# First block's gated layers: the high part of w against both parts of x in one product of 512 columns

## The chip, the cores and the metric

The kernel runs on one NeuronCore of a Trainium2 chip. The metric is device time in microseconds (us) of one execution; lower is better. Three executions of the kernel before gave 2074.72, 2075.59 and 2077.48 us; the median, 2075.59, is the time that the change is measured against.

In this document PE is the matrix engine (TensorE) and PEld its loading of weights, DVE is VectorE, ACT is ScalarE, POOL is GpSimd, SP is SyncE (it issues most DMAs). PSUM is the memory that PE writes to, in 8 banks of 512 float32 columns for each partition.

## The reference, cut to what matters

Two transformer blocks of two layers each run one after the other over x, 256 tokens of width 1024, in float32. The change touches only the gated layers of the first block: two in each of its two layers, four in all.

```python
D_MODEL, SEQ, D_FF, DEPTH = 1024, 256, 2816, 2

def rms_norm(x, g):
    xf = x.astype(jnp.float32)
    y = xf * lax.rsqrt(jnp.mean(xf * xf, axis=-1, keepdims=True) + EPS)
    return (y * g.astype(jnp.float32)).astype(x.dtype)

def swiglu(x, w_gate, w_up, w_down):
    return (jax.nn.silu(x @ w_gate) * (x @ w_up)) @ w_down

for l in range(DEPTH):
    x = x + 0.5 * swiglu(rms_norm(x, norm_ffn1[l]), w_ffn1_gate[l], w_ffn1_up[l], w_ffn1_down[l])
    x = x + hybrid_mixer(rms_norm(x, norm_mix[l]), ...)
    x = x + 0.5 * swiglu(rms_norm(x, norm_ffn2[l]), w_ffn2_gate[l], w_ffn2_up[l], w_ffn2_down[l])
```

The factor of the norm, one number r for each token, commutes with the product by a weight: (r x g) W = r ((x g) W). So it can be put on after the product, and for the up half, which enters linearly, even after w_down.

## The kernel before, in words

**Arithmetic.** Every float32 product of a weight w and an activation x is made of three products of the type fp32r: w and x are each split into a high part (a cast) and a low part (the rest), and wh·xh + wh·xl + wl·xh are summed in PSUM. The tiles are called wh, wl, xh and xl.

**The stream of weights.** All weights lie in one plan (`gated_plan`, line 585, `accum_plan`, line 417, and others) of tiles of 128 x 1024 float32, 512 KB each. `fetch` (line 354) does three things in the order of the plan: SP issues the DMA of a tile into one of 5 buffers `raw` (NRAW), ACT casts it to `wh`, DVE subtracts to get `wl` (6 buffers of each, NSPLIT). `take` (line 395) gives a split tile to the code that multiplies, `free` (line 403) says that its last product is written out, so that its buffers may be filled again.

**The order.** Every engine runs its instructions in the order in which the program wrote them. That order is planned while the program is built: `Meter` (line 111) keeps a modelled clock of each engine, `tick` (line 295) is called after every few products and lets waiting tasks (generators, `begin`) write their next step when their inputs are ready by that clock, and lets `fetch` write casts and splits. `Meter.key` (line 126) decides which parts of a tile the model tells apart.

**A gated layer.** `norm` (line 531) transposes x, multiplies by the gains and writes xh (ACT) and xl (DVE) into two tiles of 8 x 2 x 128 columns, made in `new_xT` (line 522): 8 slices k of the model dimension, 2 halves of the tokens. It then takes the mean square (ACT `junk`, POOL `xv`, `xr`: the factor r for each token), and a small product `pt<-ident,xr` on PE spreads r over the partitions; ACT copies it into the tile `factor`, 128 tokens at a time.

`gated` (line 593) runs over 11 blocks of 256 columns of w_gate and w_up. A block takes four weight tiles (two halves of k for gate and up in turn). With one tile it makes, for 2 column groups f and 4 slices k, a product wh·xh and one wh·xl of 256 columns (all tokens), then 8 products wl·xh of 256 columns: 24 products for each tile, 96 for each block, 1056 for each layer. The sums of a half (gate or up) lie in one bank: 256 columns for each f. A block holds two banks, from the rings named in `tags`: two banks each of "ps" and "pq", four of "px", so that up to four blocks have banks at one time.

`activated` (line 632) is the task that takes a block out of PSUM: for each half DVE multiplies the bank by `factor` (tile `up`), ACT does Silu on the gate half (`act` in `ffn`, line 652), DVE multiplies the halves, ACT casts the result to `h`, DVE subtracts to get `hl`.

`accum` (line 460) multiplies h and hl by the 22 tiles of w_down, in products of 512 columns (tile `acc`, the whole of "ps" and "pq"), and `residual` (line 687) adds half of the sum to x with DVE. During the last five tiles the next phase's `norm` begins. `conv_ffn` (line 659) uses the same `gated` for the second block. All instructions are recorded through one helper, line 191, so the rows are told apart by the names of their tiles.

Of the kernel before, what the change touches and what calls it, by code (L numbers as in the profile page):

```python
# [10 lines left out]
F32R = mybir.dt.float32r  # L11
# [3 lines left out]
ALU = mybir.AluOpType  # L15
AX = mybir.AxisListType

P = 128
D = 1024
S = 256  # L20
NT = 2
DFF = 2816
DEPTH = 2
KD = D // P
# [86 lines left out]
class Meter:  # L111
# [14 lines left out]
    def key(self, ap):  # L126
        name = ap.tensor.name
        div = self.cut.get(name)
        return name if div is None else (name, ap.offset // div % 2)

    def of(self, aps):
        return max((self.data.get(self.key(a), 0.0) for a in aps), default=0.0)
# [84 lines left out]
NRAW, NSPLIT, AHEAD, PACE = 5, 6, 4, 2.0  # L217
# [5 lines left out]
class Builder:  # L223
# [233 lines left out]
                        self.tick()  # L457
            k0, first = k, 1

    def accum(self, hT, kn, after, scale=1.0, tail=NSPLIT - 1):  # L460


        acc = [None, None]
        W = {}

        def mm(k, t, bs=(0, 1)):
            ah, al = hT(k, t)
            if acc[t] is None:
                acc[t] = [self.ps(f"acc{t}{b}", ("ps", "pq")[t]) for b in range(2)]
            wh, wl = W[k]  # L470
            for b in bs:
                c = slice(b * 512, (b + 1) * 512)
                self.mm3(acc[t][b], ah, al, wh[:, 0, c], wl[:, 0, c], k == 0, k == kn - 1)
                if t == NT - 1 and b == 1:
                    self.free()
                self.tick()

        for k in range(kn - tail):
            W[k] = self.take(1, D)
            for t in range(NT):  # L480
                mm(k, t)
        for t in range(NT):
            self.halves[t] = 0
        after(0)
        after(1)
        quarters = [(0, 0), (0, 1), (1, 0), (1, 1)] if self.rows_next else [(0, 0), (1, 0), (0, 1), (1, 1)]
        for i, (t, b) in enumerate(quarters):
            for k in range(kn - tail, kn):
                if i == 0:
                    W[k] = self.take(1, D)  # L490
                mm(k, t, (b,))
            self.residual(t, b, acc[t][b], scale)


    def rstd_of(self, ss, n, eps, cols=1):
# [24 lines left out]
        return r  # L520

    def new_xT(self):
        self.xh = self.cp.tile([P, KD, NT, P], F32R, tag="xh", name="xh")
        self.xl = self.cp.tile([P, KD, NT, P], F32R, tag="xl", name="xl")
        for x in (self.xh, self.xl):
            self.meter.cut[x.tensor.name] = P
        self.rstd = [None, None]
        self.ready_xT = [0, 0]
        self.factor, self.factored = [], []
# [60 lines left out]
                    self.plan.append((self.rows_of(w, k0 * P, 4, c0 + f0, 2 * P), 4, 2 * P))  # L590
        self.accum_plan(wd, 0, DFF // P)

    def gated(self, act, after, scale):


        hT, factor, factored = {}, self.factor, self.factored
        tags = ("ps", "pq", "px", "px", "ps", "pq", "px", "px", "ps", "px", "px")
        for i in range(DFF // P // 2):
            ps = [self.ps("cf", tags[i]) for half in range(2)]
            for k0 in (0, 4):  # L600
                for half in range(2):
                    self.need(lambda: min(self.ready_xT) > k0 // 4)
                    wh, wl = self.take(4, 2 * P)
                    xs = [[x[:, k0 + k].rearrange("p t f -> p (t f)") for x in (self.xh, self.xl)] for k in range(4)]

                    def mm(f, k, w, x, first=False, last=False):
                        self.nc.tensor.matmul(ps[half][:, f * S:(f + 1) * S], w[:, k, f * P:(f + 1) * P], x, start=first,
                                              stop=last, skip_group_check=True)

                    for f in range(2):  # L610
                        for k in range(4):
                            mm(f, k, wh, xs[k][0], k0 + k == 0 and f == 0)
                            mm(f, k, wh, xs[k][1])
                            if k % 2:
                                self.tick()
                    for f in range(2):
                        for k in range(4):
                            mm(f, k, wl, xs[k][0], last=k0 + k == KD - 1)
                            if f == 1 and k == 3:
                                self.free()  # L620
                            if k == 3:
                                self.tick()
            self.begin(self.activated(act, i, ps, hT, factor, factored))

        def get(k, t):
            self.need(lambda: k // 2 in hT)
            o = k % 2 * S + t * P
            return [h[:, o:o + P] for h in hT[k // 2]]

        self.accum(get, DFF // P, after, scale)  # L630

    def activated(self, act, i, ps, hT, factor, factored):

        nc = self.nc
        yield lambda: len(factored) == NT
        yield factor
        R = factor[0][:, None, :S].to_broadcast([P, 2, S])
        u = []
        for half in range(2):
            u.append(self.u("up"))  # L640
            nc.vector.tensor_tensor(u[half].rearrange("p (f s) -> p f s", f=2), ps[half].rearrange("p (f s) -> p f s", f=2),
                                    R, ALU.mult)
        yield from act(i, u)
        yield
        nc.vector.tensor_tensor(u[0], u[0], u[1], ALU.mult)
        h, lo = self.u("h", F32R), self.u("hl", F32R)
        nc.scalar.copy(h, u[0])
        yield
        nc.vector.tensor_tensor(lo, u[0], h.bitcast(F32), ALU.subtract)
        hT[i] = h, lo  # L650

    def ffn(self, after):
        def act(i, u):
            yield [u[0]]
            self.nc.scalar.activation(u[0], u[0], AF.Silu)

        self.gated(act, after, 0.5)

    def conv_ffn(self, l, after):

# [25 lines left out]

    def residual(self, t, b, acc, scale=1.0):
        xv = self.half(t, b)
        if scale == 1.0:
            self.nc.vector.tensor_tensor(xv, acc, xv, ALU.add)  # L690
        else:
            self.nc.vector.scalar_tensor_tensor(xv, acc, scale, xv, ALU.mult, ALU.add)
        self.halves[t] = b + 1
# [1154 lines left out]
```

## Time and profile before

| what | value |
|---|---|
| median of the three executions | 2075.59 us |
| the profiled execution's own time | 2073.28 us |
| its span, first to last instruction | 2071.3 us |
| what lies around the span | 1.98 us |
| PE busy | 2013.7 us (97%) |
| PEld busy | 1776.8 us (86%) |
| DVE busy | 1394.7 us (67%) |
| ACT busy | 1043.6 us (50%) |
| POOL busy | 149.8 us (7%) |

The profile is of one execution. PE is busy nearly all the time, but a product stands in the records from its issue to its end, and products overlap, so busy time says little of how fast PE goes. What counts is the distance from the start of one product to the start of the next.

### The profile page before, as it was taken

What the parts mean: (1) busy time and instruction counts of PE and PEld (TensorE: products, weight loads), DVE (VectorE), ACT (ScalarE), POOL (GpSimd) and SP (SyncE); (2) the same over time, 40 slices, a digit from 0 to 9 for tenths busy, and PEclk for the clock granted to TensorE, in tenths of its full rate; (3) what the DMA queues carried; (4) which work ended last, traced back from release to release, by engine and by line L of the source; (5) the groups of instructions that cost most, each with busy time, mean ns of one, the idle gap of its engine ahead of it and who ended that gap; (6) DMA issues with size and microseconds to landing.
All of it is one profiled execution on the core that took longest, in us unless ns stands there. A gap on an engine that the chain in (4) does not pass through costs nothing. (4 is left out here: it accounts for less than half of the span.)

```text
span 2071.3 us, 33930 instructions
## 1 busy us (share of the span) xinstructions
PE 2013.7 (97%) x13548; PEld 1776.8 (86%) x13548; DVE 1394.7 (67%) x2101; ACT 1043.6 (50%) x1605; POOL 149.8 (7%) x168
## 2 busy tenths in 40 slices
PE   8999999999999999999999999999999999999998
PEld 8998878998999887799887777889988877789997
DVE  6665666664666467666567957669955886667983
ACT  5444675443444366544455434456636444446652
POOL 0000000000000010000021031210001003110000
PEclk9999999999999999999999999999999999999999
DMA  9655623656655562356653434555664453465562
GB/s 315 195 181 152 213 83 113 198 177 194 218 180 185 157 214 92 122 174 193 186 175 114 147 112 136 180 162 177 191 200 134 133 153 98 153 192 176 177 194 97
DMA packets 246733, 343.98 MB, mean 166 GB/s; under 512 B 22064, under 2 KB 182192, under 8 KB 246448
## 3 DMA queue, kind: packets, MB, share of 16 engines
q1 hardware_dynamic: 244224, 340.20, 52.8%
q8 instruction: 106, 1.74, 0.4%
q10 hardware_dynamic: 2352, 1.63, 0.3%
q14 instruction: 51, 0.42, 0.1%
HBM read 339.68 MB, written 2.10 MB: 165 GB/s over the span
## 5 line engine op out<-in xcount | busy, mean ns | idle before, releaser
L191 DVE TENSOR_TENSOR wl<-raw,wh 128x1024 fp32r<-128x1024 f32 (+1 forms) x614 | 750.8, 1236 | 323.9 <-ACT wh L191 323.0
L191 ACT CAST wh<-raw 128x1024 fp32r<-128x1024 f32 (+1 forms) x614 | 639.3, 1046 | 585.9 <-PE cf L191 179.6
L191 PE MATMUL cf<-xh,wh 128*128 128x256 f32 x2112 | 524.7, 285 | 2.4 <-ACT wh L191 2.4
L191 PE MATMUL cf<-xl,wh 128*128 128x256 f32 x2112 | 523.0, 285 | 0.0
L191 PEld LDWEIGHTS cf<-xh,wh 128*128 128x128 f32 x2112 | 409.3, 194 | 3.0 <-ACT wh L191 2.8
L191 PEld LDWEIGHTS cf<-xl,wh 128*128 128x128 f32 x2112 | 409.2, 194 | 0.2
L191 PE MATMUL cf<-xh,wl 128*128 128x256 f32 x2112 | 300.3, 285 | 0.0
L191 PEld LDWEIGHTS cf<-xh,wl 128*128 128x128 f32 x2112 | 275.3, 194 | 0.0
L191 PE MATMUL pj<-wh,xh 128*128 128x512 f32 (+1 forms) x544 | 223.0, 410 | 4.5 <-DVE gate L191 2.0
L191 PE MATMUL pj<-wl,xh 128*128 128x512 f32 (+1 forms) x544 | 211.1, 388 | 0.0
L191 PE MATMUL pj<-wh,xl 128*128 128x512 f32 (+1 forms) x544 | 210.4, 387 | 0.0
L191 PE MATMUL acc<-wh,h 128*128 128x512 f32 x528 | 207.0, 392 | 0.0
L191 PE MATMUL acc<-wh,hl 128*128 128x512 f32 x528 | 205.6, 389 | 0.0
L191 PE MATMUL acc<-wl,h 128*128 128x512 f32 x528 | 205.5, 389 | 0.0
L191 PEld LDWEIGHTS pj<-wh,xh 128*128 128x128 f32 x544 | 102.8, 189 | 36.7 <-issue 9.9
L191 DVE TENSOR_TENSOR up<-cf,factor 128x512 f32<-128x512 f32 x132 | 90.6, 688 | 56.3 <-PE cf L191 56.2
L191 PEld LDWEIGHTS pj<-wh,xl 128*128 128x128 f32 x544 | 102.8, 189 | 21.4
L191 PEld LDWEIGHTS pj<-wl,xh 128*128 128x128 f32 x544 | 103.1, 189 | 16.9 <-DVE wl L191 0.9
L191 PEld LDWEIGHTS acc<-wh,hl 128*128 128x128 f32 x528 | 99.1, 188 | 20.9
L191 PEld LDWEIGHTS acc<-wh,h 128*128 128x128 f32 x528 | 99.2, 188 | 20.0
L191 PEld LDWEIGHTS acc<-wl,h 128*128 128x128 f32 x528 | 99.2, 188 | 19.9
L191 POOL TENSOR_SCALAR xv<-ss 128x1 f32<-128x1 f32 x24 | 20.2, 840 | 1142.6 <-ACT junk L191 1142.6
(314 smaller groups left out, 2489.6 us busy)
## 6 DMA issues: line engine op xcount, KB each, us to landing
raw<-w_in SPq DMA_DIRECT2D x156, 512.0 KB, 4.3
raw<-w_ffn_gate SPq DMA_DIRECT2D x88, 512.0 KB, 4.4
raw<-w_ffn_up SPq DMA_DIRECT2D x88, 512.0 KB, 4.8
raw<-w_ffn_down SPq DMA_DIRECT2D x88, 512.0 KB, 4.2
raw<-ffn_w_up SPq DMA_DIRECT2D x88, 512.0 KB, 4.7
raw<-ffn_w_down SPq DMA_DIRECT2D x44, 512.0 KB, 4.5
raw<-w_out SPq DMA_DIRECT2D x32, 512.0 KB, 3.7
raw<-w_branch SPq DMA_DIRECT2D x24, 512.0 KB, 4.5
```

Source lines behind the costliest of these rows:

```text
L191: return f(*args, **kw)
```

## The change

The two tiles xh and xl become one tile xx of 8 x 2 x 2 x 128 columns, so that for each slice k the 256 columns of xh and the 256 of xl lie side by side. In the first nine of the eleven blocks of a gated layer of the first block (`wides`), wh·xh and wh·xl become one product of 512 columns: it fills a whole bank, high sums in the first 256 columns and low sums in the last 256. The products wl·xh stay at 256 columns and add to the first half of the bank. Such a block has four banks (one for each half and f) in place of two: even blocks use "ps" and "pq", odd blocks the four of "px". Blocks 9 and 10 keep the old products, with banks of "px".

To take such a block out (`summed`), ACT copies the low sums of each bank to SBUF (128 x 256, four times a block) and DVE adds the high sums to them (128 x 256, four times). The factor of the norm is multiplied in only on the gate half, for a wide block by one more DVE instruction in SBUF. The up half goes on without its factor; half of it, 0.5 r, is made by two small POOL instructions in each layer (`halves`) and used in `residual` as a column of scales in place of the number 0.5. In blocks 9 and 10 the up half is read straight from PSUM by the product of the halves. The second block's `conv_ffn` passes no `wides` and no `rows` and keeps its instructions.

```diff
--- before.py
+++ after.py
@@ -126,7 +126,7 @@
     def key(self, ap):
         name = ap.tensor.name
         div = self.cut.get(name)
-        return name if div is None else (name, ap.offset // div % 2)
+        return name if div is None else (name, ap.offset // div % 4)
 
     def of(self, aps):
         return max((self.data.get(self.key(a), 0.0) for a in aps), default=0.0)
@@ -457,7 +457,7 @@
                         self.tick()
             k0, first = k, 1
 
-    def accum(self, hT, kn, after, scale=1.0, tail=NSPLIT - 1):
+    def accum(self, hT, kn, after, scale=1.0, tail=NSPLIT - 1, rows=None):
 
 
         acc = [None, None]
@@ -489,7 +489,7 @@
                 if i == 0:
                     W[k] = self.take(1, D)
                 mm(k, t, (b,))
-            self.residual(t, b, acc[t][b], scale)
+            self.residual(t, b, acc[t][b], rows[t] if rows else scale)
 
 
     def rstd_of(self, ss, n, eps, cols=1):
@@ -520,10 +520,9 @@
         return r
 
     def new_xT(self):
-        self.xh = self.cp.tile([P, KD, NT, P], F32R, tag="xh", name="xh")
-        self.xl = self.cp.tile([P, KD, NT, P], F32R, tag="xl", name="xl")
-        for x in (self.xh, self.xl):
-            self.meter.cut[x.tensor.name] = P
+        self.xx = self.cp.tile([P, KD, 2, NT, P], F32R, tag="xx", name="xx")
+        self.meter.cut[self.xx.tensor.name] = P
+        self.xh, self.xl = self.xx[:, :, 0], self.xx[:, :, 1]
         self.rstd = [None, None]
         self.ready_xT = [0, 0]
         self.factor, self.factored = [], []
@@ -590,27 +589,38 @@
                     self.plan.append((self.rows_of(w, k0 * P, 4, c0 + f0, 2 * P), 4, 2 * P))
         self.accum_plan(wd, 0, DFF // P)
 
-    def gated(self, act, after, scale):
+    def gated(self, act, after, scale, wides=(), rows=None):
+
 
 
         hT, factor, factored = {}, self.factor, self.factored
         tags = ("ps", "pq", "px", "px", "ps", "pq", "px", "px", "ps", "px", "px")
         for i in range(DFF // P // 2):
-            ps = [self.ps("cf", tags[i]) for half in range(2)]
+            two = i in wides
+            if two:
+                ps = [[self.ps("cf", ("ps", "pq")[half] if i % 2 == 0 else "px") for f in range(2)] for half in range(2)]
+            else:
+                tag = "px" if wides else tags[i]
+                ps = [[self.ps("cf", tag)] for half in range(2)]
             for k0 in (0, 4):
                 for half in range(2):
                     self.need(lambda: min(self.ready_xT) > k0 // 4)
                     wh, wl = self.take(4, 2 * P)
                     xs = [[x[:, k0 + k].rearrange("p t f -> p (t f)") for x in (self.xh, self.xl)] for k in range(4)]
-
-                    def mm(f, k, w, x, first=False, last=False):
-                        self.nc.tensor.matmul(ps[half][:, f * S:(f + 1) * S], w[:, k, f * P:(f + 1) * P], x, start=first,
-                                              stop=last, skip_group_check=True)
+                    both = [self.xx[:, k0 + k].rearrange("p z t f -> p (z t f)") for k in range(4)]
+
+                    def mm(f, k, w, x, first=False, last=False, n=S):
+                        o = ps[half][f][:, :n] if two else ps[half][0][:, f * S:(f + 1) * S]
+                        self.nc.tensor.matmul(o, w[:, k, f * P:(f + 1) * P], x, start=first, stop=last,
+                                              skip_group_check=True)
 
                     for f in range(2):
                         for k in range(4):
-                            mm(f, k, wh, xs[k][0], k0 + k == 0 and f == 0)
-                            mm(f, k, wh, xs[k][1])
+                            if two:
+                                mm(f, k, wh, both[k], k0 + k == 0, n=2 * S)
+                            else:
+                                mm(f, k, wh, xs[k][0], k0 + k == 0 and f == 0)
+                                mm(f, k, wh, xs[k][1])
                             if k % 2:
                                 self.tick()
                     for f in range(2):
@@ -620,29 +630,49 @@
                                 self.free()
                             if k == 3:
                                 self.tick()
-            self.begin(self.activated(act, i, ps, hT, factor, factored))
+            self.begin(self.activated(act, i, ps, hT, factor, factored, rows is not None))
 
         def get(k, t):
             self.need(lambda: k // 2 in hT)
             o = k % 2 * S + t * P
             return [h[:, o:o + P] for h in hT[k // 2]]
 
-        self.accum(get, DFF // P, after, scale)
-
-    def activated(self, act, i, ps, hT, factor, factored):
+        self.accum(get, DFF // P, after, scale, rows=rows)
+
+    def summed(self, o, ps, R):
+
+        if len(ps) == 1:
+            v = ps[0].rearrange("p (f s) -> p f s", f=2)
+            if R is None:
+                return v
+            self.nc.vector.tensor_tensor(o, v, R, ALU.mult)
+        else:
+            for f in range(2):
+                self.nc.scalar.copy(o[:, f], ps[f][:, S:])
+            for f in range(2):
+                self.nc.vector.tensor_tensor(o[:, f], ps[f][:, :S], o[:, f], ALU.add)
+            if R is not None:
+                self.nc.vector.tensor_tensor(o, o, R, ALU.mult)
+        return o
+
+    def activated(self, act, i, ps, hT, factor, factored, later):
+
 
         nc = self.nc
         yield lambda: len(factored) == NT
         yield factor
         R = factor[0][:, None, :S].to_broadcast([P, 2, S])
-        u = []
+        F = "p (f s) -> p f s"
+        u, v = [], []
         for half in range(2):
-            u.append(self.u("up"))
-            nc.vector.tensor_tensor(u[half].rearrange("p (f s) -> p f s", f=2), ps[half].rearrange("p (f s) -> p f s", f=2),
-                                    R, ALU.mult)
+            u.append(None if later and half and len(ps[half]) == 1 else self.u("up"))
+            v.append(self.summed(u[half] and u[half].rearrange(F, f=2), ps[half], None if later and half else R))
         yield from act(i, u)
         yield
-        nc.vector.tensor_tensor(u[0], u[0], u[1], ALU.mult)
+        if later:
+            nc.vector.tensor_tensor(v[0], v[0], v[1], ALU.mult)
+        else:
+            nc.vector.tensor_tensor(u[0], u[0], u[1], ALU.mult)
         h, lo = self.u("h", F32R), self.u("hl", F32R)
         nc.scalar.copy(h, u[0])
         yield
@@ -654,7 +684,16 @@
             yield [u[0]]
             self.nc.scalar.activation(u[0], u[0], AF.Silu)
 
-        self.gated(act, after, 0.5)
+        rows, rstd, factored = [], self.rstd, self.factored
+
+        def halves():
+            yield lambda: len(factored) == NT
+            for t in range(NT):
+                rows.append(self.small("rh", 1))
+                self.nc.gpsimd.tensor_scalar(rows[t], rstd[t], 0.5, 0.0, ALU.mult, ALU.add)
+
+        self.begin(halves(), 0)
+        self.gated(act, after, 0.5, range(9), rows)
 
     def conv_ffn(self, l, after):
 
@@ -686,7 +725,7 @@
 
     def residual(self, t, b, acc, scale=1.0):
         xv = self.half(t, b)
-        if scale == 1.0:
+        if type(scale) is float and scale == 1.0:
             self.nc.vector.tensor_tensor(xv, acc, xv, ALU.add)
         else:
             self.nc.vector.scalar_tensor_tensor(xv, acc, scale, xv, ALU.mult, ALU.add)
```

## Rows read from the trace of the kernel before

**Rows 1.** The page: span, and busy time and share of PE.

```profile
span 2071.3 us, 33930 instructions
PE 2013.7 (97%) x13548; PEld 1776.8 (86%) x13548; DVE 1394.7 (67%) x2101; ACT 1043.6 (50%) x1605; POOL 149.8 (7%) x168
```

**Rows 2.** Busy time by stretch: the second gated layer, six steady blocks of the first.

```profile
core 0: us, PE busy (x) PEld busy (x) DVE busy (x) ACT busy (x) POOL busy (x), PEclk, DMA share, GB/s
338.27:470.90 132.63, 129.39 (x1065) 129.14 (x1064) 85.13 (x92) 64.77 (x81) 4.09 (x4) 0.99 0.58 183
54.60:123.70 69.10, 69.10 (x578) 69.10 (x577) 44.40 (x48) 31.46 (x36) 0.26 (x2) 1.00 0.59 185
```

**Rows 3.** Timeline of PE (start, duration): products of 256 columns, seventeen starts in one tile.

```profile
55.60 0.28 PE L191 MATMUL cf<-xh,wh 128*128 128x256 f32 x1
...
57.52 0.28 PE L191 MATMUL cf<-xh,wl 128*128 128x256 f32 x1
```

**Rows 4.** Timeline of PE: first and last of 264 products of 512 columns.

```profile
2003.99 0.40 PE L191 MATMUL acc<-wh,h 128*128 128x512 f32 x1
...
2063.63 0.39 PE L191 MATMUL acc<-wh,hl 128*128 128x512 f32 x1
```

**Rows 5.** DVE's groups from 54.60 to 123.70: busy, mean ns | idle before, releaser.

```profile
L191 DVE TENSOR_TENSOR wl<-raw,wh 128x1024 fp32r<-128x1024 f32 x24 | 28.8, 1222 | 14.9 <-ACT wh L191 14.9
L191 DVE TENSOR_TENSOR up<-cf,factor 128x512 f32<-128x512 f32 x12 | 8.3, 688 | 5.0 <-PE cf L191 5.0
L191 DVE TENSOR_TENSOR up<-up 128x512 f32<-128x512 f32 x6 | 4.2, 693 | 0.6
L191 DVE TENSOR_TENSOR hl<-up,h 128x512 fp32r<-128x512 f32 x6 | 4.2, 693 | 4.1 <-ACT h L191 4.1
```

**Rows 6.** ACT's cast of weights in the same stretch.

```profile
L191 ACT CAST wh<-raw 128x1024 fp32r<-128x1024 f32 x24 | 25.1, 1046 | 32.5 <-PE cf L191 22.0 <-issue 10.5
```

**Rows 7.** Groups of the whole run, shapes apart: prices near those of added work.

```profile
L191 ACT COPY pts<-pt 128x256 f32<-128x256 f32 x24 | 7.7, 373 | 11.1 <-PE pt L191 11.0
L191 DVE TENSOR_TENSOR X<-pS,X 32x256 f32<-32x256 f32 x24 | 10.2, 423 | 11.3 <-PE pS L191 10.7
L191 DVE SCALAR_TENSOR_TENSOR x<-acc,x 128x512 f32<-128x512 f32 x16 | 11.1, 692 | 4.7 <-PE acc L191 4.6
L191 DVE SCALAR_TENSOR_TENSOR x<-x,xr,grow 128x512 f32<-128x512 f32 x8 | 5.7, 748 | 6.5 <-POOL xr L191 6.5
L191 POOL TENSOR_SCALAR xv<-ss 128x1 f32<-128x1 f32 x24 | 20.2, 840 | 1142.6 <-ACT junk L191 1142.6
```

**Rows 8.** Timeline of PE: the first tokens' factor in the four layers.

```profile
17.11 0.49 PE L191 MATMUL pt<-ident,xr 128*128 128x128 f32 x2 [0.79 <-POOL xr L191]
...
345.98 0.64 PE L191 MATMUL pt<-ident,xr 128*128 128x128 f32 x2 [3.24 <-POOL xr L191]
...
539.30 0.49 PE L191 MATMUL pt<-ident,xr 128*128 128x128 f32 x2 [2.15 <-POOL xr L191]
...
870.78 0.49 PE L191 MATMUL pt<-ident,xr 128*128 128x128 f32 x2 [3.24 <-POOL xr L191]
```

**Rows 9.** Second layer, second tokens' factor: POOL's xr, ACT's copy.

```profile
348.63 0.56 POOL L191 TENSOR_TENSOR xr<-xv,mh 128x1 f32<-128x1 f32 x1
...
352.55 0.27 ACT L191 COPY factor<-pt 128x128 f32<-128x128 f32 x1 [3.09 <-PE pt L191]
```

**Rows 10.** First layer: DMA by stretch, the eighth tile's cast, PE's first product with it.

```profile
20.00:31.50 11.50, 11.50 (x98) 11.50 (x98) 6.00 (x7) 5.45 (x8) 0.19 (x1) 1.00 1.08 363
...
29.99 1.05 ACT L191 CAST wh<-raw 128x1024 fp32r<-128x1024 f32 x1 [2.64 <-DMA raw<-w_ffn_up]
...
32.56 0.28 PE L191 MATMUL cf<-xh,wh 128*128 128x256 f32 x1
```

**Rows 11.** Timeline of PE: the second and the eighth product of the kernel's first block.

```profile
8.86 0.41 PE L191 MATMUL cf<-xl,wh 128*128 128x256 f32 x1
...
10.14 0.41 PE L191 MATMUL cf<-xl,wh 128*128 128x256 f32 x1
```

## The prediction

> **What bounds the kernel now.** I read the page first: PE is busy 97% of the span, the next engine 67% [rows 1]. That doesn't yet say that PE is the limit, so I went to the busy time by stretch. In the second gated layer PE is busy 129.39 of 132.63 us, and in six steady blocks of the first layer all of 69.10 us, while DVE works 44.40 and ACT 31.46 [rows 2]. The 3.24 us missing in the second layer are one wait, seen below. So in these layers the end is set by how fast PE starts one product after another, and the timeline gives that. In a weight tile the starts of products of 256 columns go from 55.60 to 57.52 in 16 steps [rows 3]: 120.0 ns each, the wl products no different from the wh ones. In the product by w_down, where every product has 512 columns, the starts go from 2003.99 to 2063.63 in 263 steps [rows 4]: 226.8 ns each. Twice the columns cost 106.8 ns more, so some 13 ns of each product are a fixed part that doesn't grow with the columns. The granted clock is 0.99 to 1.00 in these stretches, so both spacings belong to the upper level, 2.4 GHz.
>
> **The products.** A block has 4 tiles with 8 pairs of wh·xh and wh·xl each: 32 pairs. A pair becomes one product of 512 columns: 2 x 120.0 - 226.8 = 13.2 ns less. Nine blocks in four layers make 36 blocks and 1152 pairs: 1152 x 13.2 ns = 15.2 us. The wl products stay as they are. A steady block goes from 96 x 120 ns = 11.52 us to 11.10 us. The stationary operand and the type are fp32r in both rows, and the 512 columns of xx lie next to each other as those of the w_down tile do, so I take the row as it is.
>
> **Pairs that gain nothing.** The second to the eighth product of the kernel lie 0.21 us apart (8.86 to 10.14 in six steps) [rows 11]. How a product of 512 columns goes there no row shows, so I count some six pairs of 1152 as gaining nothing: 0.1 us.
>
> **Pairs ahead of a stall.** In all four layers PE stands still for the first tokens' factor, a small product that waits for POOL's xr: 0.79, 3.24, 2.15 and 3.24 us [rows 8]. What PE gains before this point it loses in the wait, since POOL's chain doesn't get faster. Between a layer's first product and the stall lie 12 to 16 pairs, some 0.2 us in each layer: 0.8 us in sum. The second tokens' factor has room: POOL's xr ends at 349.19, ACT copies the result of PE only at 352.55 [rows 9]. The bounds: where these small products stand among the others is decided by the planner in steps of a few products, and one step of two wide products (0.45 us) earlier or later in each of four layers gives 0.8 ± 1.8 us; I keep 0.8, since the planner's clock changes by little.
>
> **The start of the first layer.** Here DMA is the limit: its share is 1.08 at 363 GB/s [rows 10]. The eighth tile's cast waits 2.64 us for its DMA, ends at 31.04, and PE's first product with it starts at 32.56 [rows 10]. PE would come 0.6 us sooner (some 45 pairs), and 0.9 us of the 1.5 remain. If all four of block 0's new ACT copies stood ahead of that cast (4 x 0.373 us by the nearest copy of that shape from PSUM [rows 7]) PE would wait 0.6 us here, and as much again at a neighbour. Bounds 0 and 1.5; I take 0.3, nearer to zero, since ACT stands idle for those 2.64 us and can do the copies then.
>
> **Taking a block out.** ACT gets four copies of 256 columns: 1.5 us a block, on 31.46 / 6 = 5.2: 6.7 of 11.10. DVE loses two multiplications of a bank (2 x 0.688 [rows 5]) and gets four sums of 256 columns, one operand in PSUM (0.423 each by the nearest row [rows 7]), and one multiplication of the gate half (0.69): 7.4 - 1.4 + 1.7 + 0.7 = 8.4 of 11.10. Both fit, so I cost them at nothing. What hides them is the reserve of split weights: `fetch` lets the split run up to four tiles ahead, 11 us of PE's work. If that cover were gone, each microsecond by which DVE's work and waits pass 11.10 in a block would cost 36 us in all; that is the first rival. The step that writes the four copies and five DVE instructions has no pause inside, so the sums stand in DVE's queue until ACT has done the copies, and the copies stand behind a weight cast that often waits for PE to free a buffer (22.0 us over 24 casts [rows 6]). Behind the sums wait the next splits, and PE waits for those, but with the reserve between. Blocks 9 and 10 lose one DVE instruction each, which nothing was waiting for.
>
> **Banks.** A wide block holds four of eight, so the bank of block i must be empty when block i+2 starts, 11.10 us after block i ends. The copies and sums are 1.5 + 1.7 us of work, so they end well within that time. No wait.
>
> **The residual.** A column of scales in place of a number: 0.692 us against 0.748 for the nearest form with a column [rows 7], 0.06 more. Of four in a layer only the last has no products beside it: 4 x 0.06 = 0.2 us; all sixteen would be 0.9. POOL's two instructions a layer (0.84 each by the like of `xv` [rows 7]) come behind the second xr, and are needed 120 us later: nothing. The joined tile xx makes the first product of a layer need xl one product (0.12 us) sooner; PE then stands at its first product instead of its second, which costs nothing.
>
> **The sum.** -15.2 + 0.1 + 0.8 + 0.3 + 0.2 = -13.8 us. Against the profiled execution: 2073.28 - 13.8 = 2059.5. The median of the runs is 2.3 us above that execution (0.11%), so on its scale 2061.8. With every cost at its lower bound the gain is 16.1, at its upper bound (0.1, 2.6, 1.5, 0.9) it is 10.1: 2059.5 to 2065.5. The three runs spread by 1.4 us about their middle, which widens this to 2058.5 to 2067.
>
> **A page that speaks against it.** The fixed part of 13 ns is read from this trace [rows 3, 4]. The Trainium skill, "TensorE: Matmul & The Clock Gate", section "Back-to-back issue gap", puts the fixed part of a product at the full clock at some 2.5 ns (262 cycles for 256 columns, 518 for 512). By that figure a pair would save 2.5 ns and the change an estimated 2.9 us before its costs. The rows here contradict it for fp32r products.
>
> **Rivals.** (1) *DVE sets the pace, slower.* Today DVE idles 69.10 - 44.40 = 24.7 us in six blocks [rows 2], 4.1 a block, waiting for casts, for PE and for h [rows 5]. If these waits stayed beside 8.4 us of work, a block would take 12.5 instead of 11.52: 36 x 0.98 = 35 us more, 2111. The gain begins to shrink when the waits pass 2.7 us a block and the kernel is slower when they pass 3.1. For it: the sums queue behind ACT. Against it: most of these waits are DVE being early, for casts that wait for PE's buffers [rows 6], and they shrink as DVE falls behind; only the wait for h (0.7 a block) is a chain of its own. (2) *Two blocks of banks are too few.* PE stands for a bank at one block start in each layer, most likely the third, because the first block can't leave before the factor is there (352.55 in the second layer, 14 us after its first product at 338.27 [rows 2, 9]). A wait of one weight tile, 2.9 us, in four layers: 11.5 us, so 2073.3. Against it: the third block starts a whole block, 11 us, after the first one's end, and by then the factor is there. (3) *The wide product costs two narrow ones.* If xx streams slower than the w_down tile and the spacing is 240 ns, nothing is gained and the costs of 1.4 us remain: 2077. The 226.8 ns of the row [rows 4] speak against it. The page above, by its figure, would end in the same place, at an estimated 2075.6 - 2.9 + 1.4 = 2074.1.
>
> **How the numbers follow.** The forecast gets 0.86, the rivals 0.04, 0.06 and 0.04. No change means within 0.2% (4.2 us, 2071.4 to 2079.8), about what a measurement of this kernel can tell. The forecast lies wholly under that. Rival 2 is split between faster and no change, rival 3 is no change, rival 1 is slower: 0.89, 0.07, 0.04. The range 2058.5 to 2067.0 is the forecast's own and needs nothing from the rivals.
>
> **What would show it.** Right: wide `cf` products 227 ns apart and wl products still 120, a steady block of 11.1 us with PE never idle, each of the four layers some 3.4 us shorter up to its first `acc` product, DVE near 8.4 us a block with shorter waits for casts, stalls for xr longer by 0.1 to 0.3 us. Wrong: PE waiting at `cf` for wl or for a bank (rivals 1 and 2), wide products at 240 ns (rival 3), or the four layers shorter as forecast while the mixers between them got longer.

## The result, and the profile after

The changed kernel takes 2052.38 us (median of four, 2047.87 to 2054.74) against 2076.53 for the kernel before (four runs, 2074.72 to 2077.69): ratio 0.9882, 95% interval 0.9863 to 0.9901. It is 24 us faster, where the forecast's sum was 13.8, and lies below the range.

First the page of the changed kernel.

```profile
span 2050.2 us, 31944 instructions
PE 2000.0 (98%) x12396; PEld 1713.6 (84%) x12396; DVE 1410.8 (69%) x2201; ACT 1082.3 (53%) x1749; POOL 146.6 (7%) x176
```

It answers to [rows 1]: PE is still the limit, with 1152 products fewer. Where the time went is read from the timeline of PE: the distance from the first `cf` product of a gated layer to its first `acc` product, in us.

| gated layer | before | after | difference |
|---|---|---|---|
| 1 | 130.64 | 128.22 | -2.4 |
| 2 | 132.63 | 124.71 | -7.9 |
| 3 | 131.50 | 126.02 | -5.5 |
| 4 | 132.62 | 124.72 | -7.9 |
| 5 (second block, not touched) | 133.56 | 133.58 | 0.0 |
| 6 (second block, not touched) | 131.13 | 132.61 | +1.5 |

The four changed layers lost 23.7 us; the mixers between them stayed within 1 us each. But 288 pairs in each layer can't give 2.4 in one and 7.9 in another. Busy time by stretch for layers 2 and 3, to be laid beside [rows 2]:

```profile
core 0: us, PE busy (x) PEld busy (x) DVE busy (x) ACT busy (x) POOL busy (x), PEclk, DMA share, GB/s
336.16:460.87 124.71, 124.71 (x778) 112.33 (x777) 89.70 (x118) 74.71 (x117) 3.09 (x6) 1.00 0.65 195
522.16:648.18 126.02, 124.92 (x778) 112.20 (x776) 90.41 (x119) 74.00 (x116) 3.67 (x8) 1.00 0.64 197
```

In layer 2 PE now never waits: the 3.24 us of the kernel before are gone, and the granted clock is 1.00 where it was 0.99. In layer 3 a wait of 1.1 us is left of 2.15.

The products themselves, on the timeline of PE in a steady weight tile (start, duration, count):

```profile
66.10 2.00 PE L191 MATMUL cf<-xx,wh 128*128 128x512 f32 x8
67.94 1.11 PE L191 MATMUL cf<-xx,wl 128*128 128x256 f32 x8
68.89 0.40 PE L191 MATMUL cf<-xx,wh 128*128 128x512 f32 x1
```

Eight wide products take 1.84 us, 230 ns each and not 226.8 [rows 4]; the narrow ones still take 0.95, 119 ns. A tile takes 2.79 us instead of 2.88: 0.087 us less by the unrounded starts, where the forecast had 8 x 13.2 ns = 0.106.

Taking the blocks out, over 55.85 us (five steady blocks): busy time, then groups of DVE and of ACT:

```profile
60.51:116.36 55.85, 55.85 (x330) 49.47 (x329) 42.06 (x61) 33.18 (x55) 0.25 (x2) 1.00 0.71 215
...
L191 DVE TENSOR_TENSOR wl<-raw,wh 128x1024 fp32r<-128x1024 f32 x21 | 25.5, 1220 | 5.4 <-ACT wh L191 5.4
L191 DVE TENSOR_TENSOR up<-cf,up 128x256 f32<-128x256 f32 x24 | 9.0, 418 | 8.1 <-ACT up L191 8.1
...
L191 ACT COPY up<-cf 128x256 f32<-128x256 f32 x24 | 7.1, 380 | 0.0
```

The sums and copies cost what the nearest rows said (418 and 380 ns each [rows 7]), and DVE works 8.4 us a block, as forecast. DVE now waits 8.1 us for the copies, but its waits for casts fell from 14.9 us in six blocks [rows 5] to 5.4 in five, as a DVE that is less early would show it.

The stall is the larger part. Here is the start of layer 2 in the changed kernel, rows of ACT, POOL and PE:

```profile
340.55 0.62 ACT L191 CAST xx<-xg 128x512 fp32r<-128x512 f32 x1 [1.38 <-DVE xg L191]
341.08 0.63 ACT L191 ACTIVATE junk<-x 128x512 bf16<-128x512 f32 x1
...
342.51 0.30 POOL L191 TENSOR_SCALAR xv<-ss 128x1 f32<-128x1 f32 x1 [118.26 <-ACT junk L191]
342.90 0.57 POOL L191 TENSOR_TENSOR xr<-xv,mh 128x1 f32<-128x1 f32 x1
...
343.80 0.38 PE L191 MATMUL pt<-ident,xr 128*128 128x128 f32 x2
```

and in the kernel before, with two of the products behind the stall of [rows 8] and the clock in the stretches behind it:

```profile
341.18 0.63 ACT L191 ACTIVATE junk<-x 128x512 bf16<-128x512 f32 x1
...
342.62 1.84 POOL L191 TENSOR_SCALAR xv<-ss 128x1 f32<-128x1 f32 x1 [116.20 <-ACT junk L191]
342.67 0.62 ACT L191 CAST xh<-xg 128x512 fp32r<-128x512 f32 x1 [0.15 <-DVE xg L191]
...
344.54 1.39 POOL L191 TENSOR_TENSOR xr<-xv,mh 128x1 f32<-128x1 f32 x1
...
346.85 0.41 PE L191 MATMUL cf<-xh,wh 128*128 128x256 f32 x1
347.06 0.41 PE L191 MATMUL cf<-xl,wh 128*128 128x256 f32 x1
```

```profile
346.00:348.00 2.00, 2.00 (x10) 2.00 (x11) 0.64 (x1) 1.34 (x5) 0.00 (x0) 0.55 1.00 331
348.00:350.00 2.00, 2.00 (x13) 2.00 (x13) 0.01 (x1) 1.20 (x3) 0.86 (x2) 0.60 1.01 348
```

Two things changed. The planner wrote the mean square of the first tokens behind the cast of the second tokens, no longer ahead of it, and the factor's product later in PE's order: before, PE came to it 4.5 us after the layer's first product (342.74 - 338.27) and stood until POOL was done; now it comes 7.6 us after it (343.80 - 336.16) and finds the factor there. POOL itself is done hardly sooner, 7.3 us after the first product (342.90 + 0.57 - 336.16) where it was 7.7, so in this layer it is PE's coming later that takes the stall away. And before, the stall cost more than its own 3.24 us: after it the granted clock was 0.55 and 0.60 for some 4 us, with products 0.21 us apart, which is 256 columns at the lower level of 1.2 GHz.

### The profile page after: what moved, and what is told of

Its sections match the earlier page's. It is cut to its first block, busy times and chain, and to the rows that moved or that the text cites. A ratio compares the mean times of both kernels' runs of the same rounds, so it can differ in the third digit from the quotient of the medians.

```text
span 2050.2 us, 31944 instructions
## 1 busy us (share of the span) xinstructions
PE 2000.0 (98%) x12396; PEld 1713.6 (84%) x12396; DVE 1410.8 (69%) x2201; ACT 1082.3 (53%) x1749; POOL 146.6 (7%) x176
## 5 line engine op out<-in xcount | busy, mean ns | idle before, releaser
L191 PE MATMUL cf<-xx,wh 128*128 128x256 f32 (+1 forms) x3072 | 546.1, 326 | 2.4 <-ACT wh L191 2.4
L191 PEld LDWEIGHTS cf<-xx,wh 128*128 128x128 f32 x3072 | 449.3, 192 | 39.6 <-ACT wh L191 2.8
L191 PE MATMUL pj<-wh,xx 128*128 128x512 f32 (+1 forms) x1088 | 365.7, 398 | 4.6 <-DVE gate L191 2.0
L191 PE MATMUL cf<-xx,wl 128*128 128x256 f32 x2112 | 297.8, 284 | 0.2 <-DVE wl L191 0.2
L191 PEld LDWEIGHTS cf<-xx,wl 128*128 128x128 f32 x2112 | 282.5, 192 | 11.8 <-DVE wl L191 0.6
L191 PEld LDWEIGHTS pj<-wh,xx 128*128 128x128 f32 x1088 | 203.8, 189 | 57.8 <-issue 10.1
L191 PE MATMUL pj<-wl,xx 128*128 128x512 f32 (+1 forms) x544 | 210.4, 387 | 0.0
L191 PEld LDWEIGHTS pj<-wl,xx 128*128 128x128 f32 x544 | 102.9, 189 | 16.7 <-DVE wl L191 1.0
L191 PE MATMUL pj<-xx,wh 128*128 128x256 f32 x448 | 88.4, 297 | 1.5 <-DVE xx L191 1.0
L191 DVE SCALAR_TENSOR_TENSOR cs<-up,conv,cs 128x255 f32<-128x255 f32 (+1 forms) x176 | 77.2, 481 | 0.6
```

Source lines behind the costliest of these rows:

```text
L191: return f(*args, **kw)
```

## The experiments

Theory A, formed from these rows: about half of the gain is the pairs, the other half is the stall and the clock behind it, which went because the planner ordered the work anew. Rival B: the wide products make it all. Rival C: the joined tile or its bookkeeping alone does it.

**The planner's bookkeeping put back.** The number that the planner's key takes is 2 again in place of 4; high and low part of xx are then one entry, so a planned wide product waits for the last write of the low part, as the products with xl did before. With 4 it doesn't: its access begins in the high part, and `key` books it under that entry alone.

```diff
-        return name if div is None else (name, ap.offset // div % 4)
+        return name if div is None else (name, ap.offset // div % 2)
```

> The changed kernel with one number back: the planner's bookkeeping again tells apart only the two halves of the tokens of the x tile, not also its high and low part, so that in the plan a wide product waits for the last write of the low part too. In PE's order the first tokens' factor product then stands behind 3.7 us of a layer's products in the second and fourth gated layer, not behind 6.9; everything else is as in the changed kernel. Theory A (the gain beyond the pairs is the stall for the factor, which the planner's new order avoids, with the low clock that follows it): the stalls of 3.2 us come back in the second and fourth layer, some 4.7 us each with the clock, and about 1 us in the third: 2052.4 + 10.4 = 2063, within 3. Rival B (the wide products alone make the gain; the place of the factor product is immaterial): 2052.4, within 3.

Measured: 2059.83 us (2056.66 to 2060.16), ratio to its own runs of before (2075.27) 0.9926, interval 0.9913 to 0.9938. Some 7.5 us of the gain go by one digit that touches no arithmetic (8.7 if each kernel is held against its own runs of before). On PE's timeline the stalls are back, with the clock behind them:

```profile
343.48 0.80 PE L191 MATMUL pt<-ident,xr 128*128 128x128 f32 x2 [3.30 <-POOL xr L191]
...
532.72 0.49 PE L191 MATMUL pt<-ident,xr 128*128 128x128 f32 x2 [1.10 <-POOL xr L191]
...
859.60 0.80 PE L191 MATMUL pt<-ident,xr 128*128 128x128 f32 x2 [3.30 <-POOL xr L191]
...
343.40:345.40 2.00, 1.92 (x6) 1.64 (x7) 0.73 (x1) 1.09 (x4) 0.02 (x1) 0.50 0.87 251
```

Layers 2 and 4 take 129.64 and 130.89 us, 4.9 and 6.2 more than in the changed kernel; layer 3 is as it was, 126.01, so its shorter stall has another cause than the bookkeeping. The rows of layer 3 show which, in the kernel before and then in the changed one:

```profile
535.85 1.92 POOL L191 TENSOR_SCALAR xv<-ss 128x1 f32<-128x1 f32 x1 [186.66 <-ACT junk L191]
537.86 1.39 POOL L191 TENSOR_TENSOR xr<-xv,mh 128x1 f32<-128x1 f32 x1
```

```profile
525.82 1.38 POOL L191 TENSOR_SCALAR xv<-ss 128x1 f32<-128x1 f32 x1 [177.87 <-ACT junk L191]
527.28 0.85 POOL L191 TENSOR_TENSOR xr<-xv,mh 128x1 f32<-128x1 f32 x1
...
528.19 0.49 PE L191 MATMUL pt<-ident,xr 128*128 128x128 f32 x2 [1.10 <-POOL xr L191]
```

PE comes to the factor 4.9 us after the layer's first product in both, but POOL's two instructions take 2.2 us instead of 3.3, and the wait is shorter by that. What makes them shorter there was not tested.

The time is 3 us under what I expected. In the profiled execution the stretches from the first `acc` product of layers 4 and 5 to the next layer's first product are 3.6 us shorter in sum than in the changed kernel (370.2 and 370.7 us, against 372.2 and 372.3), and the second block's two gated layers 2.5 us. The digit changes no arithmetic there either; why they are shorter was not followed. Rival B falls.

**The joined tile alone.** The tile xx and the finer bookkeeping, without `wides` and without `rows`.

```diff
-        self.begin(halves(), 0)
-        self.gated(act, after, 0.5, range(9), rows)
+        self.gated(act, after, 0.5)
```

> The kernel before with the joined tile xx and the finer bookkeeping alone: products of 256 columns, the factor of the norm on both halves, banks as before. The factor product keeps its place in PE's order (3.8 us of products ahead of it in the second layer). Theory A: as the kernel before, 2076.5 within 2, with stalls of 3.2, 2.2 and 3.2 us. Rival C (the joined tile or the finer bookkeeping by itself takes the stall away): 2066 or less.

Measured: 2073.29 us (2072.42 to 2079.03), ratio 0.9996, interval 0.9987 to 1.0005: no change. The stalls are those of the kernel before (second row: layer 3):

```profile
346.06 0.80 PE L191 MATMUL pt<-ident,xr 128*128 128x128 f32 x2 [3.23 <-POOL xr L191]
539.13 0.49 PE L191 MATMUL pt<-ident,xr 128*128 128x128 f32 x2 [2.15 <-POOL xr L191]
```

Rival C falls. By the code, narrow products that read xl keep the planned wait under the finer bookkeeping too, and wide products under the coarse one have it as well; only both together lose it. The two runs agree: only with both is the old order gone.

**The stall taken out of both kernels.** The two factor products of all six gated layers are held until the fourth weight tile of the layer has been taken.

```diff
+            if held is not None:
+                yield lambda: held[0] >= 4
             if not self.factor:
                 self.factor.append(self.u("factor"))
...
                     wh, wl = self.take(4, 2 * P)
+                    self.held[0] += 1
```

In the kernel before:

> The kernel before, in which the two factor products of each gated layer (both blocks' layers) are held back until the layer's fourth weight tile has been taken: 9.1 us of products stand ahead of them. No arithmetic changes. Theory A: the stalls of 3.2, 2.2 and 3.2 us and the clock lost behind them (some 1.4 us each) go in layers two to four, and those of 3.2 us in the second block's two layers too: 4.7 + 3.6 + 4.7 + 4.7 + 3.2 to 4.7 = some 21 us less, 2055 within 3. Rival B (the stall only moves: PE then waits for banks, or for splits that queue behind a later evacuation): 2072 to 2077.

and in the changed one:

> The changed kernel with the same holding back of the factor products until the fourth weight tile. Theory A: only the stalls that the change left go: 1.1 us with some clock in the third layer, 3.2 us and 1.4 of clock in each of the second block's two layers: some 10 us less, 2042 within 3. Rival B (with banks for only two blocks, a first block that leaves PSUM later makes PE wait for a bank at the third block, or its evacuation comes in front of splits that PE needs): 2052 or slower.

Measured: 2052.33 us (2051.51 to 2054.14) for the first, ratio 0.9894, interval 0.9880 to 0.9907; 2039.56 (2037.94 to 2041.70) for the second, ratio 0.9831, interval 0.9818 to 0.9845. Without any change to the arithmetic, the order alone takes the kernel before to the time of the changed one. That the two times are the same is chance: on the trace the four layers are 14.2 us shorter, the second block's two layers, whose stalls the given change leaves in place, 9.4, and the stretches between them 4.5 longer. Layers 2 to 6 of it take 127.63 to 127.69 us, all alike; layers 2 to 4 of the second take 124.65 to 124.75. So the products and all that comes with them are worth 2052.33 - 2039.56 = 12.8 us by the medians. The number to hold against it is the forecast without the 0.8 that it gave to the stalls: 14.6. Of the 23.7 us in the table, 11.3 are the layers' difference between these two runs (513.24 to 501.94) and 12.4 the stalls: the four layers lost 14.2 us by them in the kernel before (527.39 - 513.24), 1.7 in the changed one (503.67 - 501.94).

**The factor on both halves.** Wide products with the held factor, but without `rows`: `gated(act, after, 0.5, range(9))`.

> The changed kernel with the held factor products, and the factor of the norm on both halves again (no scales in the residual): DVE gets one more multiplication of 0.69 us in each block, 9.1 of 11.2 us. If DVE's room covers the work of taking a block out, this costs nothing on the path: 2039.6 within 2, the four layers at 124.7 us each. Rival (DVE is so near its limit that the move of the factor to the residual is what lets the wide products pay): 36 blocks x 0.3 to 0.7 us more, 2050 to 2065.

Measured: 2046.21 us (2044.81 to 2050.84), ratio 0.9861, interval 0.9843 to 0.9880. Neither expectation: layers 2 to 4 are as with `rows` (124.75, 124.59, 124.74), but the first takes 135.36 instead of 127.80. There PE waits for the split low part; the waits of PE and the stretch 43.00 to 54.50 of this run, and then that stretch with `rows`:

```profile
PE cf L191 <- DVE wl L191: 6.7, 4, 2.9
...
43.00:54.50 11.50, 9.25 (x55) 8.24 (x56) 7.30 (x9) 4.88 (x7) 0.00 (x0) 1.00 0.70 226
```

```profile
43.00:54.50 11.50, 11.50 (x69) 10.16 (x69) 9.90 (x13) 7.08 (x11) 0.00 (x0) 1.00 0.93 304
54.50:66.00 11.50, 11.50 (x69) 10.16 (x68) 11.38 (x16) 8.56 (x13) 0.25 (x2) 1.00 0.80 239
```

With `rows` DVE is busy 11.38 of 11.50 us a little later, so it just keeps up; with one multiplication more in each block it doesn't. Between the two kernels the multiplication, 0.69 us of DVE a block, is the only work added; what goes is two small POOL instructions a layer and the column of scales in the residual. So the multiplication is most likely what tips the first layer; how the order there turns it into four waits of 6.7 us and a longer layer still was not followed further.

**The move of the factor without wide products.** The kernel before with the held factor and `gated(act, after, 0.5, (), rows)`.

> The kernel before with the held factor products and only the second half of the change: the factor of the up half moves to the residual, all products stay at 256 columns. DVE loses one multiplication of a bank in each block (the up half goes from PSUM straight into the product of the halves) and the residual takes a column of scales. If that work was hidden in the kernel before, nothing changes: 2052.3 within 2, the layers at 127.6 and the first at 130.3. Rival (DVE's work counts in the first layer even with narrow products, where the weights come late): the first layer 1 to 3 us shorter.

Measured: 2051.30 us (2050.22 to 2054.18), ratio 0.9889, interval 0.9873 to 0.9906: as without it (2052.33). The layers take 130.47, 127.63, 127.75 and 127.62 us. Alone, the move is worth nothing.

**All eleven blocks wide.** `range(11)`, held factor.

> The changed kernel with the held factor products and all eleven blocks wide. 64 pairs more in each of four layers at 10.9 ns: 2.8 us less, 2036.8, if the last block (even, in the banks that the product by w_down takes next) is out of PSUM in time. Rival: it isn't, and PE waits some 2 to 3 us at the start of each product by w_down: 2045 to 2049.

Measured: 2043.85 us (2043.04 to 2045.22), ratio 0.9847, interval 0.9832 to 0.9862, some 4 us more than with nine. On the traces the four layers account for 2.0 of them: layers 2 to 4 take 125.1 to 125.2 instead of 124.7 although they have 64 wide pairs more. The product by w_down waits for its banks, four times by up to a microsecond:

```profile
PE acc L191 <- DVE up L191: 4.0, 4, 1.0
```

The direction of the rival is right; its waits of 2 to 3 us came out at 1.0. Leaving two blocks narrow is worth it.

**Wide products in the second block too.** `conv_ffn` with `range(9)`, the factor on both halves there, held factor.

> The changed kernel with the held factor products, and wide products in nine blocks of the second block's two gated layers too, where the convolution keeps the factor of the norm on both halves. DVE works 10.6 us a block there already and gets some 1.5 more: 12.1, over the 11.2 that PE would need and over the 11.5 it needs now. My theory (DVE sets the pace there, the mechanism of the first rival of the prediction): 18 blocks x 0.6 = 11 us more, 2050, PE waiting for wl in cf. If DVE's work overlaps so far that it keeps up: 6 us less, 2033.

Measured: 2033.75 us (2030.93 to 2035.42), ratio 0.9793, interval 0.9775 to 0.9811. My theory fell: the two layers take 124.74 us, as the others do. DVE's groups in layer 5 (1342.66 to 1467.40) show why, first with wide products and then the same layer with narrow ones:

```profile
L191 DVE TENSOR_TENSOR wl<-raw,wh 128x1024 fp32r<-128x1024 f32 x46 | 55.1, 1219 | 1.9 <-ACT wh L191 1.9
...
L191 DVE TENSOR_TENSOR cs<-cs 128x512 f32<-128x512 f32 x6 | 4.1, 686 | 0.6 <-ACT cs L191 0.6
```

```profile
L191 DVE TENSOR_TENSOR wl<-raw,wh 128x1024 fp32r<-128x1024 f32 x47 | 56.8, 1220 | 1.9 <-ACT wh L191 1.9
...
L191 DVE TENSOR_TENSOR cs<-cs 128x512 f32<-128x512 f32 x10 | 6.9, 693 | 0.4 <-ACT cs L191 0.4
```

All splits are made in time, but the product of the halves has been done for six of the eleven blocks when the layer's own products end, not for ten. DVE does fall behind, in the work that nobody waits for yet, and makes it up during the product by w_down, which takes h in order of the blocks. This is the fastest kernel of the study, ahead of the kernel before and the changed one.

**Wide and narrow in turn.** In a tile a narrow product follows each wide one.

```diff
                             if two:
                                 mm(f, k, wh, both[k], k0 + k == 0, n=2 * S)
+                                mm(f, k, wl, xs[k][0], last=k0 + k == KD - 1)
```

> The changed kernel with the held factor products, where in a weight tile each wide product is followed at once by the narrow one of the same slice (512, 256, 512, 256 columns) instead of eight wide and then eight narrow ones. It asks why a tile takes 2.79 us and not the 8 x 0.2268 + 8 x 0.120 = 2.774 that the spacings of the kernel before give. If going from narrow to wide costs something each time, the tile gets longer by some 0.1 to 0.2 us. If wide products just take 0.229 to 0.230 in this stage, it stays at 2.79. If the spacing was only that of the first wide products after the narrow ones for a cause that a change of order removes, it falls to 2.77.

Measured: 2041.32 us, a single run, which can't be told from the 2039.56 (2037.94 to 2041.70) without the turn about. Layers 3 and 4 take 124.20 and 124.10 us; layers 1 and 2 take 129.72 and 125.77. In steady blocks of layer 4 five wide starts are 1.73 us apart, 0.346 for a pair, 2.77 for a tile: the forecast's spacing. In steady blocks of layers 1 and 2 of the same execution they are 1.77 apart (the second pair of rows, from layer 2), at a granted clock of 1.00 in both.

```profile
899.87 0.39 PE L191 MATMUL cf<-xx,wh 128*128 128x512 f32 x1
...
901.60 0.40 PE L191 MATMUL cf<-xx,wh 128*128 128x512 f32 x1
```

```profile
372.09 0.40 PE L191 MATMUL cf<-xx,wh 128*128 128x512 f32 x1
...
373.86 0.40 PE L191 MATMUL cf<-xx,wh 128*128 128x512 f32 x1
```

**All together.** Wide products in six layers, held factor, in turn from the third block on.

> All that the runs point to, in one kernel: the changed kernel, factor products held until the fourth weight tile, wide products in nine blocks of the second block's two gated layers too, and from the third block of each layer on a wide and a narrow product in turn. Against the run with wide products in all six layers (2033.75) the turn about saves 28 tiles x 18 ns = 0.5 us in each of six layers: 2030.7 within 2, the layers at 124.2. If the split low part, now needed at a tile's start, is late there, the layers get longer than 124.7.

Measured: 2038.46 us (2035.22 to 2039.01), ratio 0.9822, interval 0.9807 to 0.9836: slower than without the turn about. Layers 2 to 6 take 125.58 to 125.68, 0.9 more each than without it. No wait of PE for wl stands behind it; each pair takes longer, five in 1.77 us, 0.354 each:

```profile
925.92 0.40 PE L191 MATMUL cf<-xx,wh 128*128 128x512 f32 x1
...
927.69 0.40 PE L191 MATMUL cf<-xx,wh 128*128 128x512 f32 x1
```

The same order of the same products takes 0.346 in layers 3 and 4 of the run before and 0.354 here and in layers 1 and 2 there. So the order inside a tile alone doesn't set the wide product's spacing, between 226 and 234 ns if the narrow one keeps its 120. What sets it stays open.

## Why the prediction was wrong, step by step

**What bounds the kernel** held: PE sets the pace in the gated layers before and after, by the distance of its starts.

**The products** (15.2 us forecast). Right in mechanism, one product in place of two, each with its own fixed part. The size was off: 144 tiles by 0.087 us are 12.5 us, 10.9 ns a pair and not 13.2. The row of the w_down product [rows 4] was taken as it is; in the gated layers a wide product takes 230 ns. Between the two kernels without stalls the four layers differ by 11.3.

**Pairs ahead of a stall** (0.8 us lost) is the step that failed. I read the four stalls from [rows 8], took them as fixed points and asked only what they would eat of the gain. I bounded their move by one planner step of 0.45 us, "since the planner's clock changes by little". It moved the product by 3.2 us in layers 2 and 4 (7.64 after the layer's first product, where it was 4.47), because of an edit of one digit in `Meter.key` that I read as bookkeeping; together with the wide products it removed a planned wait for the low part. The premise that POOL's chain doesn't get faster failed too: in layer 3 its two instructions were 1.1 us shorter. And I priced the stall at its idle time alone. Its price in layer 2 was 132.63 - 127.63 = 5.0 us, with the low clock behind it. The runs put the stalls at 12.4 us of the gain (5.0 each in layers 2 and 4, 2.4 in layer 3, nothing in the first), where the forecast had a loss of 0.8.

**The start of the first layer** (0.3 us): PE gained 2.4 there, with a wait for wl of 0.2 us in a tile that took 3.25 us instead of 2.79 (40.50 to 43.75). A small cost of about the size given.

**Taking a block out** (nothing) held in the changed kernel: apart from that 0.2 us PE never waits for wl in the four layers, and DVE and ACT work 8.4 and 6.6 us a block where the forecast had 8.4 and 6.7. That the reserve of splits is what hides the work was not tested by itself. But its second half, the factor moved to the residual, is most likely what keeps it so in the first layer: without it 7.6 us. I had costed that half at nothing and named no cover for it; with narrow products it is nothing.

**Banks** and **the residual** held: PE never waited for a bank with nine wide blocks, and the product by w_down takes 61.3 us in both.

**The page that speaks against it.** The Trainium skill, "TensorE: Matmul & The Clock Gate", section "Back-to-back issue gap", gives a fixed part of some 2.5 ns for each product, and calls this the gap of isolated ones: in a stream of weight loads and products, it says, both set the spacing. The products here are such a stream, each with its own load, and a pair saved 10.9 ns in it. For fp32r products of 256 and 512 columns the measurement decides against using 2.5 ns here.

**Rivals.** (1) DVE as the pace: not in the changed kernel, but real in the first layer when one more instruction is added. (2) Two blocks of banks too few: only where all eleven blocks are wide, at the end of the layer and not at its third block. (3) A wide product at 240 ns: 230, so most of the gain stayed. The case that came, an order of the planner that removes a stall, was not among them.

With the stalls set aside the forecast was near: 12.8 us measured by the medians and 11.3 by the four layers, against 14.6.

## What to carry to other kernels

When the program that writes the kernel plans its order by a model, an edit to the model's bookkeeping is an edit to the schedule: look which stalls in the trace stand at a place that the planner chose, and give each the chance to go or to grow. Price a stall of the matrix engine from the start of the wait until its products are back at their usual spacing, not by the idle time. And take such a stall out of both kernels before crediting a change with its going.

## What the runs showed of the hardware that was not expected

**The clock behind a stall varies.** In layer 6 of the kernel before, PE stands for the factor and the clock then stays at 1.00; in the changed kernel, the same wait (3.24 us in both) in the same untouched layer is followed by 4 us at 0.62. First the stretch of the stall and the one behind it in the kernel before, then in the changed one:

```profile
1877.00:1880.50 3.50, 0.34 (x3) 0.13 (x2) 3.50 (x5) 2.62 (x5) 3.21 (x2) 1.00 0.85 278
1880.50:1883.00 2.50, 2.42 (x20) 2.42 (x21) 0.73 (x1) 1.90 (x6) 0.32 (x2) 1.00 0.98 309
```

```profile
1855.00:1858.10 3.10, 0.00 (x0) 0.00 (x0) 3.10 (x4) 2.36 (x3) 3.02 (x2) 1.00 0.92 296
1860.00:1864.00 4.00, 4.00 (x24) 4.00 (x24) 1.23 (x1) 1.12 (x3) 0.87 (x2) 0.62 0.80 250
```

That is the 1.5 us by which the untouched layer 6 got longer. The price of such a wait varies in one execution too: with 3.24 us of waiting in each, layers 5 and 6 of the kernel before take 5.9 and 3.5 us more than with the factor held (127.63). It may be part of why runs of one kernel spread by several us; that was not tested.

**POOL slows beside DVE.** POOL's two instructions on one column, `xv` and `xr`, take 0.30 and 0.57 us in layer 2 of the changed kernel, where DVE stands idle, and 1.84 and 1.39 in the kernel before, where DVE's splits run beside them. The Trainium skill, "SBUF — State Buffer", section "Who interferes with whom", says that a DVE instruction with two inputs in SBUF contends with a GpSimd instruction that reads SBUF; the split of weights is one. These rows agree with it, but no run here was made to separate it from other causes.
